# A conformer and state-space block on one core: partial sums of the down projection placed in the accumulation banks, and a fixed order for two kinds of activation in the mixers

## The chip, the cores and the metric

The kernel runs on one core of one Trainium2 chip. The metric is the device time of one execution in microseconds (us), taken as the median of several runs. TensorE (PE in the profile) multiplies matrices; PEld is its weight load, VectorE is DVE, ScalarE is ACT, GpSimd is POOL, and SyncE (SP) issues loads. "POOLq", "SPq" and "ACTq" are the issue queues of DMA transfers.

## The reference, cut to what matters

One transformer-like block on 512 tokens and 1024 channels, all in float32:

```python
h = rms_norm(x, mix_pre_g)
proj = h @ w_in                       # value/gate of a convolution branch, z, xbc, dt, gates
conv_out = conformer_conv_branch(...) # gated, 31-tap depthwise convolution, layer norm, SiLU, product
ssm_out = ssd_branch(z, xbc, ...)     # 8 groups: 4-tap convolution and SiLU, decay exponentials, gating by silu(z)
mixed = (g_conv * conv_out + g_ssm * ssm_out) @ w_out
x = x + rms_norm(mixed, mix_post_g)
h = rms_norm(x, ffn_pre_g)
gt, up = split(h @ w_gate_up)         # hidden width 2816
f = (silu(gt) * up) @ w_down
x = x + rms_norm(f, ffn_post_g)
```

## The kernel before

Each float32 operand is split into a high and a low half; `mm3` (L181) issues three matmuls for one product (high by high, high by low, low by high). Weights come in strips of 128 by 1024: `w_raw` (L139) loads a strip through SP's queue into one of five "raw" buffers (two more late in the kernel), ACT copies the high half out of it (`whi`, `chi`), and the low half is made in one of two ways: DVE subtracts the high half from the raw strip, or ACT writes minus the high half and POOL issues a DMA that adds the strip from memory to it. The list `ORDER` says in which sequence the strips are loaded.

The program is written with a framework that records each instruction with its operands, decides the order of every engine's queue at compile time by a list scheduler that follows the written order and its own estimate of when operands are ready, and adds all waits. `not_before(a, b)` (L176) adds an ordering edge for that scheduler between two instructions of one engine, with no wait on the chip. At run time every engine works through its queue in order.

Three places matter here.

**The mixers** (the loop from L701 over the eight groups `g`). In each group PE forms `x`, `B` and `C` strips (`proj_x`, `proj_bc`), each followed on DVE by three taps of a four-tap convolution and on ACT by a SiLU (`conv4`, L512). `make_L` (L403) loads a table of cumulative decays through POOL's queue, masks it on POOL (L410), and applies sixteen exponentials of 128 by 128 on ACT (L416). `proj_z1` and `proj_zz` form the gate `z` and apply SiLUs straight from the accumulation banks (L547, L567, L568). ACT holds one set of function tables at a time: an `ACT_TABLE_LOAD` stands ahead of the first function of another set. Between all this, DVE works off the taps of the 31-tap convolution in portions, `conv_some(n)` (L421).

**The end of the state-space branch.** After the last group `gate("gs", i)` (L735) forms six gate strips; each `gate` ends with `conv_some(TAPS_GATE)`, five taps. Then `s4` (L668) transposes the last group's result on PE, writes its high half `yh` on ACT and its low half `yl` on DVE (L679), and `ssm_out` (L685) multiplies it with the output weights, in four quarters of two products each.

**The down projection.** The first sixteen 128-row strips of `w_down` are taken as four 2 by 2 block products (`NS2 = 4`) with seven half-size products instead of eight; the seven are named P, T, S, p, Q, q, s, and `STEPS` (L103) lists them with their index `j` in the order in which PE does them. A step `k` is an ordinary strip. `prep(key)` (L1237) makes a step's operands on DVE and ACT, `S_AHEAD = 5` steps ahead of its use; `go(key)` (L1333) issues its products. `quad` (L1312) is one step on PE: 12 matmuls of 128 by 512. Each pair of banks collects one sum: A (P, then p), C (T, then q), B (S), D_2 (Q), and B2 (s). After the last P, S and Q the sums are read out into `parts[0..2]`, and the loop at the end (L1400) finishes each of four token tiles: the last strips, adding or subtracting a part (`extra`, L1409), mean square on ACT (`mean_sq`), the product with the gain on DVE (L1412), `factor` (DVE, then a power on POOL), scaling and store.

Of the kernel before, what the change touches and what calls it, by code (L numbers as in the profile page):

```python
# [18 lines left out]
P = 128  # L19
T = 512  # L20
# [82 lines left out]
STEPS = [("P", 0), ("P", 1), ("T", 0), ("P", 2), ("S", 0), ("T", 1), ("P", 3), ("S", 1)]  # L103
STEPS += [("p", 0), ("T", 2), ("p", 1), ("S", 2), ("p", 2), ("T", 3), ("p", 3), ("S", 3)]
STEPS += [("Q", 0), ("Q", 1), ("q", 0), ("Q", 2), ("q", 1), ("Q", 3), ("q", 2)]
STEPS += [("s", 0), ("k", KS2), ("q", 3), ("s", 1), ("k", KS2 + 1), ("s", 2), ("k", KS2 + 2), ("s", 3)]
BLOCKS = {"P": ((1, 0),), "T": ((1, 1),), "S": ((1, 2),), "p": ((1, 3),), "Q": ((2, 1), (2, 2)), "s": ((2, 3),)}
# [14 lines left out]
def block_kernel(ctx: ExitStack, tc: tile.TileContext, x, xT, x0, prm, hp, gp, w, out):  # L122
# [279 lines left out]

    def make_L(g, first=None):  # L403
        L = ssd.tile([P, HG, NT, P], F32, tag="L", bufs=2, name=f"L{g}")
        Lf = L.rearrange("p h c l -> p (h c l)")
        src = scr[HG * g : HG * (g + 1)].rearrange("h c l -> (h c l)").partition_broadcast(P)
        load = pool.dma_start(Lf, src)
        if first:
            not_before(load, first)
        pool.affine_select(  # L410
            out=Lf, in_=Lf, compare_op=ALU.is_ge, fill=-1e30, base=0,
            pattern=[[0, HG * NT], [1, P]], channel_multiplier=-1,
        )
        for c in range(NT):
            for h in range(HG):
                act.activation(L[:, h, c, :], L[:, h, c, :], AF.Exp, bias=nacs[:, c, HG * g + h : HG * g + h + 1])  # L416
        return L
# [94 lines left out]
    def conv4(ps, i, name):  # L512

        a = xbc_tile(name)
        act.activation(a, ps, AF.Identity, scale=col("ssm_w", i * KS + KS - 1), bias=col("ssm_b", i))  # L515
        for d in range(1, KS):
            dve.scalar_tensor_tensor(  # L517
                out=a[:, d:], in0=ps[:, : T - d], scalar=col("ssm_w", i * KS + KS - 1 - d),
                in1=a[:, d:], op0=ALU.mult, op1=ALU.add,
            )  # L520
        act.activation(a, a, AF.Silu)
        return a
# [11 lines left out]
    def proj_z1():  # L534
# [3 lines left out]
        for t2 in range(2):  # L538
# [8 lines left out]
            act.activation(z[:, 2 * t2 : 2 * t2 + 2, :], ps.rearrange("p (a b) -> p a b", a=2), AF.Silu)  # L547
        st[1]["z"] = z

    def proj_zz(g):  # L550
# [7 lines left out]
        for t in range(NT):  # L558
# [8 lines left out]
            act.activation(zb[t // 2][:, t % 2, :], ps[:, :GW], AF.Silu)  # L567
            act.activation(z[:, t, :], ps[:, GW:], AF.Silu)  # L568
# [166 lines left out]
    def gate(n, i, out_):  # L735
# [4 lines left out]
        conv_some(TAPS_GATE)  # L740
# [13 lines left out]
    gate("gs", 5, xbc_tile("sgs5"))  # L754
    s4(G - 1)
    ssm_out(G // 2 - 1, range(4))
# [480 lines left out]
    def prep(key):  # L1237
# [26 lines left out]
        elif kind == "p":  # L1264
            w_form(key, w_of(1, j, 3), seq["w1", 4 * j + 3])
            f_form(key, b21)
        elif kind == "Q":
# [4 lines left out]
        elif kind == "q":  # L1272
            dve.tensor_tensor(out=b11, in0=b11, in1=b21, op=ALU.add)
            w_form(key, w_of(2, j, 2), seq["w2", 4 * j + 2])
            f_form(key, b11)
        elif kind == "s":
            dve.tensor_tensor(out=keep[j], in0=keep[j], in1=w_of(2, j, 3), op=ALU.add)
            w_form(key, keep[j])
            f_form(key, b22)
# [28 lines left out]
    parts = [slot(tg, [P, 2, T], f"part{i}") for i, tg in enumerate(("b22h", "b22l", "t4h"))]  # L1308
# [3 lines left out]
    def quad(key, ps, start, stop, more=False):  # L1312

        (wh, wl), (fh, fl) = Wd[key], F_[key]
        for i in range(2):
            c = slice(i * T, (i + 1) * T)
            for e in range(2):
# [6 lines left out]
    at_b = [(turn["big"] - 3 + e) % 8 for e in range(2)]  # L1324
    B2 = []

    def f_step(t, k, n):
        (wh, wl), c, before = Wd["k", k], slice(n * T, (n + 1) * T), mark["pe3"]
        fh, fl = [f[:, t % 2, t // 2 * P : (t // 2 + 1) * P] for f in F_["k", k]]
        m = mm3(ps[t][n], fh, fl, wh[:, c], wl[:, c], False, k == NF - 1, ps[t][n] not in B2)  # L1330
        not_before(m, before)

    def go(key):  # L1333
# [9 lines left out]
        elif kind == "S":  # L1343
            quad(key, B, first_, last_)
            if last_:
                for e in range(2):
                    dve.tensor_tensor(out=parts[0][:, e], in0=B[e], in1=parts[0][:, e], op=ALU.add)
                for e in range(2):
                    dve.tensor_tensor(out=parts[1][:, e], in0=C[e], in1=parts[0][:, e], op=ALU.subtract)
        elif kind == "p":  # L1350
            quad(key, A, False, False, True)
        elif kind == "Q":
            quad(key, D_2, first_, last_)
            if last_:
                for e in range(2):
                    dve.tensor_tensor(out=parts[2][:, e], in0=parts[0][:, e], in1=D_2[e], op=ALU.subtract)
        elif kind == "q":
            quad(key, C, False, False, True)
        elif kind == "s":
            if first_:  # L1360
                B2.extend(yd_tile(at_b[e], f"tm_b2{e}") for e in range(2))
                ps.update({1: (B2[0], D_2[0]), 3: (B2[1], D_2[1])})
            quad(key, B2, first_, False)
# [5 lines left out]
    ps = {0: (A[0], C[0]), 2: (A[1], C[1])}  # L1369
# [12 lines left out]
    for t, tg in zip((1, 3, 0, 2), KEEP):  # L1382
# [3 lines left out]
    extra = {  # L1386
        (1, 0): (parts[2][:, 0], ALU.add), (3, 0): (parts[2][:, 1], ALU.add),
        (1, 1): (parts[1][:, 0], ALU.add), (3, 1): (parts[1][:, 1], ALU.add),
        (0, 1): (parts[0][:, 0], ALU.subtract), (2, 1): (parts[0][:, 1], ALU.subtract),
    }  # L1390

# [8 lines left out]
    for t in (1, 3, 0, 2):  # L1400
        mg = [w2.tile([P, T], F32, tag=tg, bufs=2, name=f"mg_{tg}{t}") for tg in ("dhi", "dlo")]
        ss = []
        for n in (1, 0):
            for k in range(KS2 + 3, NF):
                f_step(t, k, n)
            of = ps[t][n]
            if (t, n) in extra:
                by, op = extra[t, n]
                dve.tensor_tensor(out=mg[n], in0=of, in1=by, op=op)  # L1409
# [91 lines left out]
```

## Time and profile before

| what | us |
|---|---|
| median of three runs (1040.8 to 1042.3) | 1042.24 |
| the profiled execution's own time | 1039.82 |
| its span, first to last instruction | 1038.0 |
| PE busy | 1022.0 |
| DVE busy | 805.8 |
| ACT busy | 632.0 |
| POOL busy | 99.8 |

The profile is of one execution. A timeline row has the start, the duration, the engine, the line, the operation with the tiles it writes and reads, the shapes, a count of merged instructions and, in brackets, idle time of the engine just before it with what ended it. A row of waits has the waiting instruction, the one that released it, the sum in us, how often, and the longest. A row of stretches has, for the stretch, busy us and count of instructions of each engine, then TensorE's granted clock as a share of full speed, the busy share of the DMA engines and GB/s. A group row has its busy time and the mean ns of one, then the idle time before and what ended it. A matmul of 128 by 512 is shown with 0.39 us, but they overlap: the next one starts 0.23 us later.

### The profile page before, as it was taken

How to read it: one execution, taken by the hardware profiler on the slowest of the kernel's cores; microseconds unless marked ns; L12 is line 12 of the kernel's file. 1: busy time of each engine (PE TensorE's matmuls, PEld its weight loads, DVE VectorE, ACT ScalarE, POOL GpSimd, SP SyncE). 2: the span in 40 equal slices, each digit the busy share in tenths (PEclk: the TensorE clock that was granted, in tenths of full speed). 3: DMA queues.
4: the chain of work that ended last, by engine and by line, in shares of the span. 5: the costliest groups of instructions: out<-in, count | busy, mean ns of one | idle time of the engine just before them, and what ended most of it. 6: DMA issues, size and time to landing. Idle time of an engine off the chain costs nothing.

```text
span 1038.0 us, 15741 instructions
## 1 busy us (share of the span) xinstructions
PE 1022.0 (98%) x6101; PEld 885.9 (85%) x6101; DVE 805.8 (78%) x1172; ACT 632.0 (61%) x1047; POOL 99.8 (10%) x124
## 2 busy tenths in 40 slices
PE   9999999999999999999999999999999999999996
PEld 7898889878888888888878888889999999988785
DVE  7899976968595969597976455479997887897925
ACT  7655988684867476735432582376665664785712
POOL 0102101110111011101100000010000000010101
PEclk9999999999999999999999999999999999999999
DMA  8567634656456554544433223434565354488902
GB/s 295 155 167 227 144 91 134 184 133 173 119 144 159 131 145 134 157 128 121 119 106 102 81 79 105 162 110 135 164 185 160 106 164 138 143 219 267 304 21 81
DMA packets 43034, 152.91 MB, mean 147 GB/s; under 512 B 4944, under 2 KB 5968, under 8 KB 41936
## 3 DMA queue, kind: packets, MB, share of 16 engines
q1 hardware_dynamic: 30960, 105.71, 29.9%
q0 software_dynamic: 9792, 39.85, 19.5%
q10 hardware_dynamic: 2208, 6.36, 1.8%
q8 instruction: 48, 0.79, 0.3%
q14 instruction: 26, 0.21, 0.1%
HBM read 147.64 MB, written 4.26 MB: 146 GB/s over the span
## 4 chain that ended last, share of the span: by engine, by line
PE 78%; issue 7%; DVE 6%; ACT 4%; DMA 2%; POOL 1%; SPq 0%; POOLq 0%; DVEq 0%; ACTq 0%
PE xy L183 3%; PE xy L184 3%; PE xy L185 3%; PE pso L184 3%; PE pso L185 3%; PE pso L183 3%; PE px L185 2%; PE px L183 2%; PE px L184 2%; PE yv L184 2%; PE pz L184 2%; PE yv L183 2%; PE pz L183 2%; PE yv L185 2%; PE pz L185 2%
## 5 line engine op out<-in xcount | busy, mean ns | idle before, releaser
L149 ACT CAST whi<-raw 128x1024 fp32r<-128x1024 f32 (+2 forms) x116 | 115.1, 1004 | 161.4 <-PE pso L184 40.1
L433 DVE SCALAR_TENSOR_TENSOR a<-v,prm_t,a 128x511 f32<-128x511 f32 (+15 forms) x240 | 180.5, 754 | 10.6 <-ACT a L430 7.9
L155 DVE TENSOR_TENSOR wlo<-raw,whi 128x1024 fp32r<-128x1024 f32 (+2 forms) x76 | 86.1, 1136 | 48.5 <-ACT whi L149 46.1
L153 POOL DMA_DIRECT2D wlo<-in_w x40 | 35.8, 894 | 359.4 <-ACT wlo L152 125.3
L184 PE MATMUL pz<-wlo,hhi 128*128 128x512 f32 (+2 forms) x160 | 56.2, 352 | 0.5 <-DVE wlo L155 0.5
L185 PE MATMUL pz<-whi,hlo 128*128 128x512 f32 (+2 forms) x160 | 56.3, 352 | 0.0
L183 PE MATMUL pz<-whi,hhi 128*128 128x512 f32 (+2 forms) x160 | 55.9, 356 | 0.0
L184 PE MATMUL pso<-yl,whi 128*128 128x512 f32 x128 | 50.0, 390 | 1.4 <-DVE yl L679 1.4
L183 PE MATMUL px<-hhi,whi 128*128 128x512 f32 x128 | 50.2, 392 | 0.0
L917 ACT CAST whi_g<-raw 128x1024 fp32r<-128x1024 f32 x40 | 41.3, 1054 | 14.4 <-DVE raw L948 7.4
L185 PE MATMUL pso<-yh,wlo 128*128 128x512 f32 x128 | 49.9, 390 | 0.0
L185 PE MATMUL px<-hhi,wlo 128*128 128x512 f32 x128 | 49.8, 389 | 0.0
L184 PE MATMUL px<-hlo,whi 128*128 128x512 f32 x128 | 49.8, 389 | 0.0
L183 PE MATMUL pso<-yh,whi 128*128 128x512 f32 x128 | 49.7, 393 | 0.0
L922 DVE TENSOR_TENSOR wlo_g<-raw,whi_g 128x1024 fp32r<-128x1024 f32 x34 | 41.2, 1220 | 5.1 <-ACT whi_g L917 5.0
L416 ACT ACTIVATE L<-L,nacs 128x128 f32<-128x128 f32 x128 | 40.1, 390 | 5.6 <-POOL L L410 5.4
L152 ACT ACTIVATE wlo<-whi 128x1024 fp32r<-128x1024 f32 x40 | 42.2, 1056 | 0.3
L517 DVE SCALAR_TENSOR_TENSOR x<-px,prm_t,x 128x511 f32<-128x511 f32 (+2 forms) x48 | 35.1, 743 | 1.4 <-ACT x L515 1.2
L184 PEld LDWEIGHTS pz<-wlo,hhi 128*128 128x128 f32 x160 | 30.1, 188 | 5.0 <-DVE wlo L155 1.3
L183 PEld LDWEIGHTS pz<-whi,hhi 128*128 128x128 f32 x160 | 30.1, 188 | 4.0
L185 PEld LDWEIGHTS pz<-whi,hlo 128*128 128x128 f32 x160 | 30.1, 188 | 3.7
L917 ACT CAST chi_g<-raw 128x1024 fp32r<-128x1024 f32 x24 | 24.9, 1052 | 10.1 <-PE yv L185 4.6
(684 smaller groups left out, 3358.4 us busy)
## 6 DMA issues: line engine op xcount, KB each, us to landing
raw<-in_w SPq DMA_DIRECT2D x188, 512.0 KB, 4.3
wlo<-in_w POOLq DMA_DIRECT2D x40, 512.0 KB, 5.7
L<-scr POOLq DMA_DIRECT2D x8, 1024.0 KB, 6.4
wlo_g<-in_w POOLq DMA_DIRECT2D x13, 512.0 KB, 8.2
clo_g<-in_w POOLq DMA_DIRECT2D x7, 512.0 KB, 6.4
xr<-in_x ACTq DMA_DIRECT2D x4, 512.0 KB, 5.7
x2d<-xr ACTq DMA_DIRECT2D x4, 512.0 KB, 2.6
xres<-x2d SPq DMA_DIRECT2D x4, 512.0 KB, 4.9
```

Source lines behind the costliest of these rows:

```text
L149: act.copy(hi[:, c], src[:, c])
L152: act.activation(lo[:, c], hi[:, c].bitcast(F32), AF.Copy, scale=-1.0)
L153: mark["lo"] = pool.dma_start(lo[:, c], w[n][:, c].bitcast(F32R), accum_op=ALU.add)
L155: mark["wlo"] = dve.tensor_tensor(out=lo[:, c], in0=src[:, c], in1=hi[:, c].bitcast(F32), op=ALU.subtract)
L183: mark["pe"] = pe.matmul(ps, lh, rh, start=start, stop=False, skip_group_check=more)
L184: pe.matmul(ps, lh, rl, start=False, stop=False, skip_group_check=more)
L185: mark["pe3"] = pe.matmul(ps, ll, rh, start=False, stop=stop, skip_group_check=more)
L416: act.activation(L[:, h, c, :], L[:, h, c, :], AF.Exp, bias=nacs[:, c, HG * g + h : HG * g + h + 1])
L433: return dve.scalar_tensor_tensor(out=va[j][:, d:], in0=vs[j][:, : T - d], scalar=col("dw_w", j * KC + KC - 1 - d), in1=va[j][:, d:], op0= ...
L517: dve.scalar_tensor_tensor(out=a[:, d:], in0=ps[:, : T - d], scalar=col("ssm_w", i * KS + KS - 1 - d), in1=a[:, d:], op0=ALU.mult, op1=ALU ...
L917: a_ = act.copy(hi, src)
L922: d_ = dve.tensor_tensor(out=lo, in0=src, in1=hi.bitcast(F32), op=ALU.subtract)
```

## The change

There are three edits.

In the **down projection** the sums are written into the accumulation banks in the middle of the work instead of being kept aside and added at the end. `C` gets C minus parts[0] by an ACT copy after the last S; `B` gets parts[0] minus D_2, and `D_2` gets D_2 plus parts[1], both by DVE after the last Q; q, s and the last strips then go on adding to these banks. The third part and the bank pair B2 are gone, and so are the six DVE instructions at the end (`extra`). The order of the steps changes: S3 stands ahead of p3, and Q2 ahead of q0. The sum of weights that step s needs is made in step p from the strip that p has loaded anyway (the fourth blocks of "w1" and "w2" hold the same data), so the four loads of "w2" for s are gone. The low half of q's weights is made by DVE and no longer by ACT and an adding DMA.

In the **mixers** every exponential of `make_L` and every SiLU of `conv4`, `proj_z1` and `proj_zz` gets an ordering edge to the one written before it.

At the **end of the state-space branch** the five taps behind the gate strip gs5 move behind the first quarter of the last `ssm_out`.

```diff
+    "P0 P1 T0 P2 S0 T1 P3 S1 p0 T2 p1 S2",
+    "p2 T3 S3 p3 Q0 Q1 Q2 q0 q1 Q3 q2 s0",
+    "k16 q3 s1 k17 s2 k18 s3",
...
-BLOCKS = {"P": ((1, 0),), "T": ((1, 1),), "S": ((1, 2),), "p": ((1, 3),), "Q": ((2, 1), (2, 2)), "s": ((2, 3),)}
+BLOCKS = {"P": ((1, 0),), "T": ((1, 1),), "S": ((1, 2),), "p": ((1, 3),), "Q": ((2, 1), (2, 2))}
...
+    def by_table(ins):
+
+        if "table" in mark:
+            not_before(ins, mark["table"])
+        mark["table"] = ins
...
-                act.activation(L[:, h, c, :], L[:, h, c, :], AF.Exp, bias=nacs[:, c, HG * g + h : HG * g + h + 1])
+                by_table(
+                    act.activation(L[:, h, c, :], L[:, h, c, :], AF.Exp, bias=nacs[:, c, HG * g + h : HG * g + h + 1])
+                )
...
-        act.activation(a, a, AF.Silu)
+        by_table(act.activation(a, a, AF.Silu))
...
-    gate("gs", 5, xbc_tile("sgs5"))
+    gate("gs", 5, xbc_tile("sgs5"), 0)
     s4(G - 1)
-    ssm_out(G // 2 - 1, range(4))
+    ssm_out(G // 2 - 1, (0,))
+    conv_some(TAPS_GATE)
+    ssm_out(G // 2 - 1, (1, 2, 3))
...
         elif kind == "p":
             w_form(key, w_of(1, j, 3), seq["w1", 4 * j + 3])
             f_form(key, b21)
+            dve.tensor_tensor(out=keep[j], in0=keep[j], in1=w_of(1, j, 3), op=ALU.add)
...
         elif kind == "q":
             dve.tensor_tensor(out=b11, in0=b11, in1=b21, op=ALU.add)
-            w_form(key, w_of(2, j, 2), seq["w2", 4 * j + 2])
+            w_form(key, w_of(2, j, 2))
             f_form(key, b11)
         elif kind == "s":
-            dve.tensor_tensor(out=keep[j], in0=keep[j], in1=w_of(2, j, 3), op=ALU.add)
             w_form(key, keep[j])
             f_form(key, b22)
...
                 for e in range(2):
                     dve.tensor_tensor(out=parts[1][:, e], in0=C[e], in1=parts[0][:, e], op=ALU.subtract)
+                    act.copy(C[e], parts[1][:, e])
...
-                    dve.tensor_tensor(out=parts[2][:, e], in0=parts[0][:, e], in1=D_2[e], op=ALU.subtract)
+                    dve.tensor_tensor(out=B[e], in0=parts[0][:, e], in1=D_2[e], op=ALU.subtract)
+                    dve.tensor_tensor(out=D_2[e], in0=D_2[e], in1=parts[1][:, e], op=ALU.add)
...
-            quad(key, B2, first_, False)
+            quad(key, B, False, False, True)
...
-            of = ps[t][n]
-            if (t, n) in extra:
-                by, op = extra[t, n]
-                dve.tensor_tensor(out=mg[n], in0=of, in1=by, op=op)
-                of = mg[n]
-            ss.append(mean_sq(of, pt, f"c{t}", n))
-            dve.tensor_tensor(out=mg[n], in0=of, in1=gpost1[:, cols2[n]], op=ALU.mult)
+            ss.append(mean_sq(ps[t][n], pt, f"c{t}", n))
+            dve.tensor_tensor(out=mg[n], in0=ps[t][n], in1=gpost1[:, cols2[n]], op=ALU.mult)
```

More of the change, by code (lines that the diff above doesn't have):

```diff
@@ L733, in block_kernel, with gate @@
     gates = {}
-    def gate(n, i, out_):
+    def gate(n, i, out_, taps_=TAPS_GATE):
         ps = mm_tile(f"p{n}{i}")
@@ L1307, in block_kernel, with quad @@
     pt = ctx.enter_context(tc.tile_pool(name="pt", bufs=1))
-    parts = [slot(tg, [P, 2, T], f"part{i}") for i, tg in enumerate(("b22h", "b22l", "t4h"))]
+    parts = [slot(tg, [P, 2, T], f"part{i}") for i, tg in enumerate(("b22h", "b22l"))]
     gpost1 = slot("t4l", [P, D], "gpost1")
     nc.scalar.dma_start(gpost1, gp[1].partition_broadcast(P))
-    def quad(key, ps, start, stop, more=False):
+    def quad(key, ps, start, stop, more=False, es=(0, 1)):
         (wh, wl), (fh, fl) = Wd[key], F_[key]
@@ L1316, in quad @@
             c = slice(i * T, (i + 1) * T)
-            for e in range(2):
+            for e in es:
                 tok = slice(e * P, (e + 1) * P)
@@ L1329, in f_step @@
         fh, fl = [f[:, t % 2, t // 2 * P : (t // 2 + 1) * P] for f in F_["k", k]]
[L1330 removed]
+        m = mm3(ps[t][n], fh, fl, wh[:, c], wl[:, c], False, k == NF - 1, True)
         not_before(m, before)
@@ L1367, in go @@
                     f_step(t, j, n)
-    ps = {0: (A[0], C[0]), 2: (A[1], C[1])}
+    ps = {0: (A[0], C[0]), 2: (A[1], C[1]), 1: (B[0], D_2[0]), 3: (B[1], D_2[1])}
     ahead = STEPS + [("k", k) for k in range(KS2 + 3, NF)]
```

26 lines of the change are left out of this document (8 added, 18 removed).

## The prediction

> **What bounds the kernel now.** I read first the page's span and busy times, then PE's waits, then the stretches in which PE is not full.
>
> ```profile
> span 1038.0 us, 15741 instructions
> PE 1022.0 (98%) x6101; PEld 885.9 (85%) x6101; DVE 805.8 (78%) x1172; ACT 632.0 (61%) x1047; POOL 99.8 (10%) x124
> ```
> ```profile
> PE tm_c L183 <- DVE part L1349: 2.3, 1, 2.3
> PE pso L184 <- DVE yl L679: 1.4, 1, 1.4
> ...
> PE pz L184 <- DVE wlo L155: 0.5, 1, 0.5
> ...
> PE pyT L677 <- ACT y L664: 0.3, 1, 0.3
> ```
> ```profile
> 208.00:234.00 26.00, 25.23 (x117) 20.39 (x116) 16.94 (x23) 21.72 (x42) 3.93 (x5) 1.00 0.56 138
> ...
> 520.00:546.00 26.00, 24.62 (x112) 19.98 (x111) 19.11 (x25) 8.31 (x10) 0.92 (x1) 1.00 0.40 109
> ...
> 962.00:988.00 26.00, 23.66 (x104) 19.17 (x104) 23.50 (x30) 19.20 (x25) 2.62 (x3) 1.00 0.91 282
> ...
> 1014.00:1040.00 26.00, 15.33 (x68) 12.33 (x66) 15.19 (x26) 5.72 (x16) 3.10 (x4) 0.87 0.22 81
> ```
>
> ```profile
> 1028.49 0.39 PE L183 MATMUL tm_a<-whi_g,fh_k 128*128 128x512 f32 x1
> 1028.72 0.39 PE L184 MATMUL tm_a<-wlo_g,fh_k 128*128 128x512 f32 x1
> 1028.94 0.39 PE L185 MATMUL tm_a<-whi_g,fl_k 128*128 128x512 f32 x1
> ```
>
> The kernel's last three matmuls: one starts every 0.23 us, so a step of 12 takes 2.74.
>
> PE is idle for 1038.0 - 1022.0 = 16.0 us in all, at a granted clock of 1.00 in the stretches that matter. The change takes no matmul away and adds none, so nothing outside these 16 us can be won, except by another order of PE's queue. Where they lie: 0.8 in the mixers (26.00 - 25.23), 1.4 at the end of the state-space branch, 2.3 in the down projection, and 24.0 - 15.33 = 8.7 in the last stretch, of which only what follows PE's last matmul counts. The change touches all four places. The rest (the start, the gate and up projection) it leaves alone.
>
> The profiled execution took 1039.82, 1.8 more than its span; it is 2.4 below the median of 1042.24 and 1.0 below the lowest run shown. I make the sum on the profiled one and carry the difference over to the median.
>
> **1. The end of the state-space branch.**
>
> ```profile
> 521.44 1.23 DVE L155 TENSOR_TENSOR wlo<-raw,whi 128x1024 fp32r<-128x1024 f32 x1 [2.65 <-ACT whi L149]
> 522.58 3.80 DVE L433 SCALAR_TENSOR_TENSOR a<-v,prm_t,a 128x495 f32<-128x495 f32 x5
> 526.29 0.75 DVE L679 SCALAR_TENSOR_TENSOR yl<-pyT,prm_t,yh 128x512 fp32r<-128x512 f32 x1
> ...
> 529.26 0.69 DVE L698 TENSOR_TENSOR so<-pso,so 128x512 f32<-128x512 f32 x1 [0.92 <-PE pso L185]
> ```
> ```profile
> 523.78 1.26 ACT L678 ACTIVATE yh<-pyT,prm_t 128x512 fp32r<-128x512 f32 x2
> ```
> ```profile
> 527.09 0.50 PE L184 MATMUL pso<-yl,whi 128*128 128x512 f32 x1 [1.38 <-DVE yl L679]
> ```
>
> `yh` is there from about 524.4 on, but DVE makes `yl` only at 526.29, behind five taps of 3.80/5 = 0.76 us. Counted in fives back from 526.29, one is the last of gs4 and four belong to gs5. Without gs5's, DVE is free at 523.4, `yl` waits for `yh` alone and ends at 524.4 + 0.75 = 525.2; PE needs it at 527.09 - 1.38 = 525.7. So the wait goes whole: -1.4. The five taps (3.8 us) come after the first quarter. DVE's queue there has idle spots (0.92 before the first sum of results), and a result of `ssm_out`, 12 matmuls of 0.23 = 2.7 us, has three banks in turn, so an evacuation may be some 5 us late. I put them at nothing; if that cover is gone they cost 3.8 - 2.7 = 1.1. Bounds: -1.4 to -0.3.
>
> **2. The down projection, wait at the first q.**
>
> ```profile
> 942.96 1.23 DVE L1269 TENSOR_TENSOR raw<-raw,raw 128x1024 f32<-128x1024 f32 x1 [2.15 <-DMA raw<-in_w]
> ...
> 947.68 1.23 DVE L1269 TENSOR_TENSOR raw<-raw,raw 128x1024 f32<-128x1024 f32 x1 [2.29 <-DMA raw<-in_w]
> ...
> 956.91 1.23 DVE L1269 TENSOR_TENSOR raw<-raw,raw 128x1024 f32<-128x1024 f32 x1 [0.46 <-DMA raw<-in_w]
> ...
> 961.00 1.22 DVE L1277 TENSOR_TENSOR keep<-keep,raw 128x1024 f32<-128x1024 f32 x1
> ...
> 966.82 1.28 DVE L1347 TENSOR_TENSOR part<-tm_b,part 128x512 f32<-128x512 f32 x2
> 968.02 1.28 DVE L1349 TENSOR_TENSOR part<-tm_c,part 128x512 f32<-128x512 f32 x2
> 969.21 1.21 DVE L1229 TENSOR_TENSOR wlo_g<-keep,whi_g 128x1024 fp32r<-128x1024 f32 x1
> ...
> 976.41 1.23 DVE L1277 TENSOR_TENSOR keep<-keep,raw 128x1024 f32<-128x1024 f32 x1 [2.50 <-DMA raw<-in_w]
> ...
> 982.76 1.28 DVE L1356 TENSOR_TENSOR part<-part,tm_d 128x512 f32<-128x512 f32 x2
> ```
> ```profile
> 968.84 0.47 PE L183 MATMUL tm_c<-whi_g,f_q 128*128 128x512 f32 x1 [2.34 <-DVE part L1349]
> ```
> ```profile
> 935.75 1.27 ACT L1340 COPY part<-tm_a 128x512 f32<-128x512 f32 x2 [0.48 <-PE tm_a L185]
> ```
>
> q0 adds to bank C, and must wait until DVE has read C (968.02). PE came at 968.84 - 2.33 = 966.51. The last S had ended two steps before, near 961: DVE read it six us late, because its queue was full of preparations, and these had stood before for strips that DMA had not brought (2.15 + 2.29 + 0.46 = 4.9 us).
>
> What the new order gives: S3 one step earlier and Q2 ahead of q0 put p3, Q0, Q1, Q2 between S3 and q0 instead of Q0, Q1. Two steps are 2 x 12 x 0.23 = 5.5 us more cover; PE reaches q0 at 966.51 + 2.74 = 969.25. What DVE gets ahead of the parts: the four sums of weights move from s into p. Two of them stood ahead of the parts anyway (961.00 is one), so two are new: 2 x 1.14 = 2.3 us (1.22, less the overlap with the next, as from 521.44 to 522.58 above). The low half of q0's weights: 1.1. What it loses there: q1's preparation, which is five steps ahead no longer: 0.6 + 1.1 + 0.6 = 2.4. Net +1.0, so the parts end at 969.2 + 1.0 = 970.2 if DMA brings nothing sooner. Then the ACT copy into C, 1.27 for both banks by the only copy of that size shown (out of a bank, not into one): the first bank at about 970, the second 0.6 later. The wait would be about 1.2.
>
> ```profile
> q1 hardware_dynamic: 3203, 11.68, 57.8%
> q0 software_dynamic: 932, 3.36, 30.8%
> ```
>
> These are the DMA queues of 935 to 990 us: packets, MB, share of all DMA engines' time. The loads cost 57.8% x 55 / 11.68 = 2.7 us a MB, the adding DMAs 30.8% x 55 / 3.36 = 5.0. Four loads and four adding DMAs of 0.52 MB go: 2.1 x 2.7 + 2.1 x 5.0 = 16 us of the 49 that the DMA engines are busy here. The strips for Q2 and later then come sooner, and some of the 4.9 us of DVE's waiting goes; the waits at 942.96 and 947.68 also simply absorb the sums moved into p. I take the wait at q0 as 0.3 instead of 2.3: -2.0. Bounds: -2.3 (no wait) to +1.2 (two sums and their strips held longer, the first wait unrelieved: 3.5 instead of 2.3).
>
> [...]
>
> **3. The down projection, a new wait at the first s.** B is written from D_2 after Q3, and s0 needs it one step (2.74) after Q3. Before, DVE read D_2 at 982.76; s0 began at 982.66 in a fresh bank. If DVE stays as late, s0 waits 0.1 + 0.64 = 0.7 for the first bank and, with D_2's own sum in between, 1.3 for the second. But DVE had lost 2.50 us for s3's strip at 976.41, which is not loaded any more, and two sums of 1.14 that moved away; it gets two subtractions for q2 and q3. That is some 2.5 us of room: I take +0.2. Bounds: 0 to +1.3.
>
> **4. The tail.**
>
> ```profile
> 1029.92 0.63 ACT L853 ACTIVATE jk_c<-mg_dlo 128x512 bf16<-128x512 f32 x1 [3.90 <-DVE mg_dlo L1409]
> ...
> 1030.96 0.60 ACT L853 ACTIVATE jk_c<-tm_a 128x512 bf16<-128x512 f32 x1 [0.32 <-ACT jk_c L853]
> ```
>
> PE's last matmul ends at 1028.94 + 0.39 = 1029.33. ACT could square the last bank then, but it begins at 1030.96: it does the other half first, which waited until 1029.92 for DVE's addition of a part. Without that addition the other half is squared as soon as its bank is done, at about 1027.3, two us before the last one. The last square begins at 1029.4: 1.6 earlier, and all behind it (product, factor, power on POOL, scaling, store) moves with it. -1.6. Bounds: -1.0 (a store of the tile before in DVE's way: one 0.6 more) to -1.9.
>
> **5. The mixers.**
>
> ```profile
> L416 ACT ACT_TABLE_LOAD x19 | 24.4, 1283 | 0.3
> L521 ACT ACT_TABLE_LOAD x14 | 18.0, 1283 | 0.3
> ```
> ```profile
> L149 ACT CAST whi<-raw 128x1024 fp32r<-128x1024 f32 (+2 forms) x116 | 115.1, 1004 | 161.4 <-PE pso L184 40.1 <-PE pC L184 22.3 <-PE pgs L184 21.8
> ```
>
> In written order each group needs one load for its exponentials and one for its SiLUs: 8 + 8 instead of 19 + 14, so ACT saves some 17 x 1.28 = 22 us. ACT is busy 632 of 1038 and hardly delays PE: of its waits only 0.8 us lie here, and the 0.5 among them wait for a weight half of DVE. I take -0.3. Bounds: -0.8 to +1.5 (a table load's worth of one cast that comes late). What covers the sixteen exponentials in one block: the casts of weights behind them. By the group row the casts wait for PE to give back a strip, 161.4 us in all, so they are strips ahead.
>
> [...]
>
> **Sum:** -1.4 - 2.0 + 0.2 - 1.6 - 0.3 = -5.1. The profiled execution would go from 1039.8 to 1034.7, the median from 1042.24 to 1037.1.
>
> **The rivals.**
>
> *A, the wait only moves* (17%). DVE is not sooner at the parts, q0 waits 1.2 to 3.5, s0 as much as above. Then 2 and 3 cancel and the rest stays: -1.4 - 1.6 = -3.0, 1039.2. For it speaks that DVE is busy 23.50 of 26 there; against it the 5.5 us of cover.
>
> *B, nothing that can be told* (12%). The scheduler lists other queues around the edits. Tail and `yl` win 3.0, and new waits of the same kind and size as those now in the list (2.3 the longest) take it back: about 1042.
>
> *C, slower: DVE's lateness feeds itself through the raw buffers* (13%). Place: p0 to the parts. The sum that moves into p makes DVE the last reader of p's strip, where ACT's cast was; a buffer comes free later, so the next load starts later, and DVE stands for it. If the four sums count whole (4.6 instead of 2.3) and DVE's 4.9 us of standing for strips doubles, the parts come at 969.2 + 1.0 + 2.3 + 4.9 = 977.4 and q0 waits 978.0 - 969.25 = 8.8: +6.4 against before; with 1.3 at s0 and the 3.0 won elsewhere, +4.7: 1047. It decides from the point where q0's wait passes 2.3 + 3.0 = 5.3. For it: the DMA share of 0.91, and the three waits. Against: the adding DMAs gone, and DVE's standing absorbs work first.
>
> That the mixers' edit does nothing (the loads don't fall in number) would cost the 0.3 only.
>
> **How the numbers follow.** Forecast 58%: 1037.1, its own range 1035 to 1039. All bounds at their best: -1.4 - 2.3 - 1.9 - 0.8 = -6.4, 1035.8, and runs scatter by 1.5 (1040.8 to 1042.3): low 1034.3. The high end takes in A and half of B: 1041.8. A measurement of this kernel can tell about 0.2%, 2.1 us. Faster by more: the forecast and A, 75%; within it: B, 12%; slower: C, 13%.
>
> **What would show it.** PE's waits: `pso` on `yl` gone; `tm_c` under 1 us, and behind DVE `part` or an ACT copy; a wait of `tm_b` on DVE (0 to 1.3). The last square of ACT starts within 0.2 us of PE's last matmul, and the span ends some 7 us after it instead of 8.7. Table loads of L416 and L521 at 16 to 20 together. Strips of L145 are four fewer, adding DMAs of L1227 four fewer. I am wrong if PE's idle time grows between 940 and 990, if the tail does not shorten, or if waits of PE for ACT or for weight halves appear in the mixers.

## The result, and the profile after

| | median, us | runs | range |
|---|---|---|---|
| before | 1042.27 | 4 | 1040.8 to 1044.42 |
| after | 1032.12 | 4 | 1031.56 to 1032.59 |

The ratio is 0.9901 (95% interval 0.9883 to 0.9919): 10.15 us gone, twice the 5.1 of the forecast, and below the range. The profiled execution took 1032.06, its span is 1030.3. The span of before's profiled execution was 1038.0, so from trace to trace only 7.7 have gone; the other 2.4 are the distance of that execution from before's median.

Some executions of most kernels here take about 6 us longer than the others (27 of 92 later ones of before, at a median of 1048.3 instead of 1042.7), in the traces all of it between 730 and 940 us, so where about half of a kernel's runs are such I also give the median of the lower ones, and the profiles of down_only, dma_kept, hold2 and old_order are of the longer kind.

The page's first lines, PE's waits, the ACT table loads among the groups, and the four stretches that answer to those of before (the last one again ends with the span):

```profile
span 1030.3 us, 15679 instructions
PE 1020.2 (99%) x6101; PEld 886.6 (86%) x6101; DVE 803.8 (78%) x1172; ACT 602.2 (58%) x1024; POOL 94.6 (9%) x120
```
```profile
PE warm_ps L270 <- DVE woken L265: 1.0, 1, 1.0
PE xy L186 <- DVE f L1107: 0.9, 2, 0.5
PE v L187 <- DVE t1l L1041: 0.4, 1, 0.4
PE yv L186 <- ACT f L1170: 0.2, 1, 0.2
```
```profile
L426 ACT ACT_TABLE_LOAD x8 | 10.3, 1283 | 0.1
L532 ACT ACT_TABLE_LOAD x8 | 10.3, 1283 | 3.2 <-DVE x L528 3.1
```
```profile
208.00:234.00 26.00, 26.00 (x121) 21.55 (x120) 13.46 (x18) 21.13 (x47) 3.93 (x5) 1.00 0.61 162
520.00:546.00 26.00, 26.00 (x120) 21.23 (x119) 19.02 (x26) 7.96 (x9) 0.92 (x1) 1.00 0.39 105
962.00:988.00 26.00, 26.00 (x116) 21.40 (x115) 21.23 (x26) 13.66 (x19) 0.00 (x0) 1.00 0.32 110
1006.00:1032.00 26.00, 17.17 (x76) 13.85 (x74) 11.40 (x20) 5.51 (x16) 2.19 (x4) 0.91 0.22 81
```

`tm_c`, `pso`, `pz` and `pyT` have left the list of waits: PE is full in the first three stretches. The table loads at these two lines are 16, against 19 + 14. In both traces a load, of 1283 ns, stands ahead of an exponential, SiLU or sigmoid wherever the one before it on ACT was of another of these three kinds, 52 times in before and 31 in after, and besides only once, at the start. The DMA share of 962 to 988 has fallen from 0.91 to 0.32.

The down projection and the tail, in order of time, from the timeline of after:

```profile
955.36 1.28 DVE L1357 TENSOR_TENSOR part<-tm_b,part 128x512 f32<-128x512 f32 x2
956.56 1.27 DVE L1359 TENSOR_TENSOR part<-tm_c,part 128x512 f32<-128x512 f32 x2
...
957.27 1.19 ACT L1360 COPY tm_c<-part 128x512 f32<-128x512 f32 x2 [0.48 <-DVE part L1359]
...
965.52 0.39 PE L186 MATMUL tm_c<-chi_g,f_q 128*128 128x512 f32 x1
...
1022.79 0.39 PE L188 MATMUL tm_a<-whi_g,fl_k 128*128 128x512 f32 x1
...
1023.45 0.60 ACT L866 ACTIVATE jk_c<-tm_a 128x512 bf16<-128x512 f32 x1 [1.54 <-PE tm_a L188]
```

The parts begin 11 us sooner than before (966.82), where the prediction had them end 1.0 later (970.2 instead of 969.2). Of the 11, 3.6 are PE's own lead when it comes to these steps; counted from the same matmul of step P3 (PE's 5700th) the parts begin 23.8 us later, in before 31.7. The copies into C end at 957.27 + 1.19 = 958.46, and q0 starts at 965.52: 7 us are to spare. From the end of PE's last matmul (1022.79 + 0.39) to the end of the span are 1030.3 - 1023.2 = 7.1 us, where before had 1038.0 - 1029.3 = 8.7. A single copy of 128 by 512 on ACT takes 0.591 into a bank (after) and 0.586 out of one (before); the 1.19 and 1.27 of the merged rows differ only in how closely the second follows the first.

### The profile page after: what moved, and what is told of

The parts are those of the page before. It is cut to its first block, busy times and chain, and to the rows that moved or that the text cites. A ratio compares the mean times of both kernels' runs of the same rounds, so it can differ in the third digit from the quotient of the medians.

```text
span 1030.3 us, 15679 instructions
## 1 busy us (share of the span) xinstructions
PE 1020.2 (99%) x6101; PEld 886.6 (86%) x6101; DVE 803.8 (78%) x1172; ACT 602.2 (58%) x1024; POOL 94.6 (9%) x120
## 4 chain that ended last, share of the span: by engine, by line
PE 91%; DVE 4%; ACT 2%; issue 1%; POOL 0%; ACTq 0%; POOLq 0%; DVEq 0%
PE xy L186 3%; PE xy L187 3%; PE xy L188 3%; PE pz L187 3%; PE pz L188 3%; PE pz L186 3%; PE pso L186 3%; PE pso L187 3%; PE px L188 3%; PE pso L188 3%; PE px L186 3%; PE px L187 3%; PE yv L186 2%; PE yv L187 2%; PE yv L188 2%; PE yd L636 2%
```

## The experiments

In the terms of the expectations, "theory T" is: listed waits, a granted clock that before loses behind its wait at the first q, and a wait in the mixers that many executions of before have and the first profile had not. Theory D looks for the whole surplus in the down projection, M for a part of it in the mixers, S in the chip or the moment.

### What each edit brings alone

The kernel before once more, and with one edit of the three at a time, on one chip.

> The kernel before, unchanged. Its profiled execution took 1039.8, the median of its runs 1042.3, up to 1044.4; the changed kernel's runs all lie within 1.0 of each other. Theory D (the down projection): what differs from run to run is how long PE waits at the first q, since the loads there fill the DMA engines; a slower execution then shows a wait of tm_c on DVE part above 2.3 us, by as much as its span is above 1038.0. Rival M (the mixers): the wait of tm_c stays at 2.3 and PE's waits between 100 and 530 us grow instead. Rival S (neither; the chip or the moment): this chip shows about 1040 with all waits of PE as in the first profile.

> The down projection's edit alone. In the traces it is worth 2.6 at the first q and 1.6 in the tail. D: it also takes away the 2.4 by which the runs lie above the profiled one: 1042.3 - 6.6 = 1035.7, ratio 0.9937, and its runs lie within 1.5 of each other. M or S: 1042.3 - 4.2 = 1038.1, ratio 0.9960, under M with the scatter of before (3 to 4 us).

> The edges between exponentials and SiLUs alone. In the traces worth 1.8 to 2.0, nearly all near 205 to 225 us, where two waits of PE (0.5 and 0.3 as listed) go. D or S: 1042.3 - 1.9 = 1040.4, ratio 0.9982, scatter as before. M: 1042.3 - 1.9 - 2.4 = 1038.0, ratio 0.9959, scatter under 1.5. In its profile some 15 to 17 table loads fewer at L416 and L521 (their lines move by a few) and neither wait.

> The five taps moved behind the first quarter, alone. By the traces 1.6 (the wait of pso on yl was listed with 1.4): 1040.7, ratio 0.9985, under D, M and S alike. If a wait cost only what the list gives, 1.4. If the taps were paid back behind the first quarter, under 0.5.

The edits are the three of the diff, each alone; before_again alters nothing.

| | median, us | ratio to before, 95% interval | lower runs |
|---|---|---|---|
| before_again | 1043.01 | 1.0002, 0.9981 to 1.0022 | |
| down_only | 1039.62 | 0.9949, 0.9925 to 0.9973 | six of 1036.04 to 1037.43, median 1036.8 |
| mixers_only | 1041.3 | 0.9968, 0.9946 to 0.999 | seven of 1037.66 to 1041.74, median 1040.3 |
| taps_only | 1041.55 | 0.9964, 0.9941 to 0.9987 | |

PE's waits in before_again:

```profile
PE tm_c L183 <- DVE part L1349: 2.0, 1, 2.0
PE pyT L677 <- ACT y L664: 1.8, 1, 1.8
PE pso L184 <- DVE yl L679: 1.4, 1, 1.4
```

The second profile of the same kernel is not the first: `pyT` waits 1.8 for ACT, where the first showed 0.3 (and 0.5 of `pz`). taps_only and down_only show 1.8 as well, mixers_only none. before_again gives a ratio of 1.0002, so S falls; the down projection's edit is the largest part, about 6 us in its lower runs, but the other two bring more than the 1.7 that the prediction gave them together, so D alone does not do either.

Of before_again, the stretches around the first q, and PE's timeline from its wait on:

```profile
964.00:968.00 4.00, 3.65 (x17) 2.68 (x15) 3.87 (x5) 4.00 (x6) 0.98 (x2) 1.00 0.87 307
968.00:972.00 4.00, 2.39 (x6) 1.95 (x7) 4.00 (x7) 3.97 (x6) 0.13 (x1) 0.70 1.02 251
972.00:976.00 4.00, 4.00 (x17) 3.25 (x16) 2.66 (x3) 1.91 (x3) 0.89 (x1) 0.87 1.05 299
```
```profile
969.61 0.75 PE L183 MATMUL tm_c<-whi_g,f_q 128*128 128x512 f32 x1 [1.96 <-DVE part L1349]
970.16 0.63 PE L184 MATMUL tm_c<-wlo_g,f_q 128*128 128x512 f32 x1
970.58 0.63 PE L185 MATMUL tm_c<-whi_g,f_q 128*128 128x512 f32 x1
971.01 0.63 PE L183 MATMUL tm_c<-whi_g,f_q 128*128 128x512 f32 x1
...
973.34 0.39 PE L183 MATMUL tm_c<-whi_g,f_q 128*128 128x512 f32 x1
973.57 0.39 PE L184 MATMUL tm_c<-wlo_g,f_q 128*128 128x512 f32 x1
```

Behind the wait of 1.96 the matmuls start every 0.43 us instead of 0.23, until 973.1, and the granted clock is 0.70 and 0.87. No wait lists this: PE counts as busy. From the wait on, 24 starts in a row took 1.7 us more than 24 x 0.228. So the wait at the first q costs about twice what it is listed with. mixers_only (3.5 of wait) lost 2.7 behind it, taps_only (2.8) 1.7. The first profile of before, with 2.34 of wait, lost 0.1 and kept a clock of 1.00: an exception among executions of before, since its mean clock of 0.998 is reached by only 4 of the 92 later runs of before (most have 0.995 or 0.996), while the changed kernel and down_only have 0.998 or 0.999 in all.

mixers_only and taps_only also show that the edits do not simply add up. In mixers_only PE comes 3.9 us sooner to the down projection than in before_again, but the parts do not come sooner by as much: the wait grows from 2.0 to 3.5 and the loss behind it from 1.7 to 2.7, and only 1.3 of the 3.9 are left at the end. In taps_only 1.6 become 0.4. And the wait of `pso` on `yl` is gone in mixers_only as well, with the five taps in their old place. Its DVE there:

```profile
516.75 1.23 DVE L155 TENSOR_TENSOR wlo<-raw,whi 128x1024 fp32r<-128x1024 f32 x1
517.89 5.34 DVE L439 SCALAR_TENSOR_TENSOR a<-v,prm_t,a 128x497 f32<-128x497 f32 x7
523.35 0.75 DVE L685 SCALAR_TENSOR_TENSOR yl<-pyT,prm_t,yh 128x512 fp32r<-128x512 f32 x1
```

Before, DVE stood 2.65 us for ACT's `whi` ahead of the last `wlo` (at 521.44); here it doesn't, and is through the taps in time. So either edit alone removes this wait. Whether the five taps' place is worth anything beside the mixers' edges was not run; by this trace it is not (PE takes 74.5 us from its 2600th to its 3000th matmul in mixers_only, in taps_only and in after, and 76.1 in before).

### What in the down projection does it

after_again alters nothing. dma_kept and dma_less are:

```diff
 after, to dma_kept
-            dve.tensor_tensor(out=keep[j], in0=keep[j], in1=w_of(1, j, 3), op=ALU.add)   # in step p
-            w_form(key, w_of(2, j, 2))
+            w_form(key, w_of(2, j, 2), seq["w2", 4 * j + 2])
+            dve.tensor_tensor(out=keep[j], in0=keep[j], in1=w_of(2, j, 3), op=ALU.add)   # in step s
```
```diff
 before, to dma_less
-STEPS += [("p", 0), ("T", 2), ("p", 1), ("S", 2), ("p", 2), ("T", 3), ("p", 3), ("S", 3)]
+STEPS += [("p", 0), ("T", 2), ("p", 1), ("S", 2), ("p", 2), ("T", 3), ("S", 3), ("p", 3)]
+            dve.tensor_tensor(out=keep[j], in0=keep[j], in1=w_of(1, j, 3), op=ALU.add)   # in step p
-            w_form(key, w_of(2, j, 2), seq["w2", 4 * j + 2])
+            w_form(key, w_of(2, j, 2))
-            dve.tensor_tensor(out=keep[j], in0=keep[j], in1=w_of(2, j, 3), op=ALU.add)   # in step s
```

> The changed kernel once more, nothing altered. Theory T (the gain is the listed waits, 5 to 6 us, plus the clock that before loses behind its wait at the first q, plus a 1.8 us wait in the mixers that most executions of before have): the granted clock is 0.998 or more in every run; the lowest runs are 1031.5 to 1033; about a third of the runs lie some 6 us higher, 1037 to 1039, as they do for before and for the down projection's edit alone, because nothing in the change touches that. Rival U (the change also removes that second level): no run above 1034.

> The changed kernel, but the low half of q's weights is again made by ACT and an adding DMA, and the four w2 strips for s are loaded and summed in step s again, so that the DMA engines keep their load of before; the order of the steps and the sums in the banks stay new. By the order alone (two steps, 5.5 us more cover for the parts) there is no wait at the first q above 0.5 us and the time is within 1.5 of the changed kernel's own. Rival (the relief of the DMA engines is what brought the parts forward): the first q waits 1 to 4 us, the granted clock dips behind it, and the time is 3 to 6 above the changed kernel's.

> The kernel before, with the relief of the DMA engines and S3 one step earlier (S3 ahead of p3, the sum of s's weights made in p from the strip that is there, the low half of q's weights on DVE); Q2 stays behind the first q, and the parts are added at the end as before, with no sum written into a bank. If earlier strips and one step of cover (2.7 us) are enough: no wait of tm_c above 0.5, granted clock 0.998 or more, 3 to 4 us below before (about 1038.5 to 1039.5), the tail 8.7 as before, the pso and pyT waits as before. Rival: the wait at the first q stays at 1 or more and the time within 1.5 of before.

after_again: 1032.71 (0.9906, 0.9882 to 0.9929), five runs of 1031.96 to 1033.27 and one of 1039.32; rival U falls. dma_kept: 1042.97 (0.9998, 0.9979 to 1.0016), no gain left at all. dma_less: 1037.88 (0.9946, 0.993 to 0.9962), six runs within 1.4 us.

dma_kept, PE's one long wait, and DVE's queue from its timeline:

```profile
PE tm_b L186 <- DVE tm_b L1367: 7.0, 1, 7.0
```
```profile
966.23 1.23 DVE L1290 TENSOR_TENSOR keep<-keep,raw 128x1024 f32<-128x1024 f32 x1 [1.33 <-DMA raw<-in_w]
...
969.71 1.28 DVE L1357 TENSOR_TENSOR part<-tm_b,part 128x512 f32<-128x512 f32 x2
...
979.29 1.23 DVE L1290 TENSOR_TENSOR keep<-keep,raw 128x1024 f32<-128x1024 f32 x1 [5.36 <-DMA raw<-in_w]
...
990.26 0.69 DVE L1367 TENSOR_TENSOR tm_b<-part,tm_d 128x512 f32<-128x512 f32 x1
```

The new order does what the prediction wanted of it: the first q does not wait, although the parts are about as late as before (969.71; counted from the same matmul of P3, 30.9 us later, in before 31.7). But the same lateness then meets the first s, where B must be written: 7.0 us. With the sums and the DMA load left in place, the order only moves the wait. The expectation of the order alone had the first q right and the time wrong; the rival had the sign, but neither the place nor the size (10.7 above after's 1032.3, where it said 3 to 6). In dma_less, with the old place of Q2 and no sum in a bank, no wait of `tm_c` is left.

Four more kernels take the relief and the order apart. old_order puts Q2 behind the first q again, q_by_dma gives q's low half back to ACT and the adding DMA, loads_kept loads the four strips of s again without using them, and strips_only is before with nothing but the sum for s moved into p (and S3 ahead of p3, as p adds to what S makes).

```diff
 after, to old_order
-    "p2 T3 S3 p3 Q0 Q1 Q2 q0 q1 Q3 q2 s0",
+    "p2 T3 S3 p3 Q0 Q1 q0 Q2 q1 Q3 q2 s0",
 after, to q_by_dma
-            w_form(key, w_of(2, j, 2))
+            w_form(key, w_of(2, j, 2), seq["w2", 4 * j + 2])
 after, to loads_kept
+            again = w_of(2, j, 3)[:, :1]            # in step s
+            pool.tensor_scalar(out=again, in0=again, scalar1=1.0, scalar2=None, op0=ALU.mult)
 dma_less, to strips_only
-            w_form(key, w_of(2, j, 2))
+            w_form(key, w_of(2, j, 2), seq["w2", 4 * j + 2])
```

> The changed kernel with Q2 behind the first q again (S3 stays ahead of p3), so one step of cover, 2.7 us, is taken from the parts. The changed kernel's parts and copies are done 7 us before the first q, so by theory T (the relief of DMA brought them forward) 4.3 us are left and the time is the changed kernel's, within 0.6. By the prediction's step 2 (the order is what hides the parts) a wait of 1 to 2.5 us comes back, and with the clock behind it the time is 1034 to 1037.

> The changed kernel, but the low half of q's weights is made by ACT and an adding DMA again; the four w2 strips for s stay away. It parts the relief of the DMA engines in two. If the four adding DMAs are the greater half of it (2.1 MB at 5.0 us a MB against 2.1 at 2.7, by the prediction): strips come late again, DVE stands for them by 3 us or more, a wait of 1 to 4 us shows at the first s or the first q, and the time is 1035 to 1038. If the four strips of s, with their sums in DVE's queue, are what holds it up: no wait above 0.5 in the down projection, and the time within 1 us of the changed kernel's.

> The changed kernel, but the four w2 strips for s are loaded again, at their old place in the sequence of loads; nothing is made of them but that POOL multiplies one column by 1.0, and the sum for s is still made in p. If the DMA engines' load and the raw buffers are what held DVE up: strips behind these come late, DVE stands for them, the first s or the first q waits several us, and the time is that of the run that kept strips and sums, near 1043. If it was DVE standing in its queue at the sums, whose strips had not come: no wait above 0.5 in the down projection and the time within 1 of the changed kernel's, 1032 to 1033.5.

> The kernel before with the sum for s made in p and the four w2 strips gone (for that S3 must stand ahead of p3, since p adds to what S makes); the low half of q's weights stays with ACT and the adding DMA, the parts are added at the end, the mixers and the five taps are as before. If the strips of s alone carry the gain: the wait of tm_c gone, granted clock 0.997 or more, and the time that of the run in which q's low half moved too, 1037.5 to 1038.5. If the adding DMAs matter as well in the old order: a wait of tm_c of 1 or more, 1040 to 1043.

| | median, us | ratio to before, 95% interval | lower runs |
|---|---|---|---|
| old_order | 1033.32 | 0.9919, 0.9886 to 0.9951 | four of 1032.79 to 1033.37 |
| q_by_dma | 1032.58 | 0.9894, 0.9868 to 0.9919 | all six |
| loads_kept | 1032.99 | 0.9901, 0.9871 to 0.9932 | all four |
| strips_only | 1041.15 | 0.9967, 0.9941 to 0.9993 | six of 1037.06 to 1038.84, median 1037.8 |

None of the four shows a wait in the down projection. So neither Q2's place nor the adding DMAs nor the four loads, each put back alone, bring the wait back (by the lower runs they cost 0.3 to 0.8); strips_only, in its lower runs, has the whole gain of dma_less (1037.88). loads_kept, its DMA queues of 935 to 990 us and DVE's timeline at the parts:

```profile
q1 hardware_dynamic: 3033, 11.04, 53.6%
```
```profile
954.53 1.22 DVE L1283 TENSOR_TENSOR raw<-raw,raw 128x1024 f32<-128x1024 f32 x1
955.67 1.28 DVE L1359 TENSOR_TENSOR part<-tm_b,part 128x512 f32<-128x512 f32 x2
```

It loads 11.04 MB there (before 11.68, after 8.93) and still has its parts at 955.67, directly behind the fourth sum for Q. In before there were ten us between these two (956.91 and 966.82), filled with preparations and with the sums for s at 961.00 and 965.08. In loads_kept it is POOL that stands for these strips, and nothing waits for POOL.

Counted from the same matmul of P3, the parts begin 31.3 to 32.9 us later in the four traces with before's down projection, 30.9 in dma_kept, and 23.3 to 24.1 in all others. Where the 8 us go is seen in strips_only, which keeps the adding DMAs and Q2's old place:

```profile
954.90 1.22 DVE L1270 TENSOR_TENSOR raw<-raw,raw 128x1024 f32<-128x1024 f32 x1
...
957.84 1.22 DVE L1229 TENSOR_TENSOR clo_g<-raw,chi_g 128x1024 fp32r<-128x1024 f32 x1
958.98 1.28 DVE L1347 TENSOR_TENSOR part<-tm_b,part 128x512 f32<-128x512 f32 x2
```

The fourth sum for Q comes 2.0 us sooner, and between it and the parts lie 4.1 us of DVE's queue instead of 9.9: the two sums for s (2.3) are gone from there, and 3.5 us of preparations are now listed behind the parts. In before DVE did not stand at those two sums themselves (961.00 has no idle time before it); it stood at the strips for Q ahead of them, and behind the parts, at 976.41, for a strip of s. In dma_kept it stands for the sums' own strips, 1.33 ahead of the parts and 5.36 behind them.

That the sums in DVE's queue are the cause is therefore likely, but not shown to the end. Only before's down projection and dma_kept have the adding DMAs and the four loads together (14.2 to 15.2 and 15.0 MB moved between 935 and 990 us); all others move 13.0 MB or less. A kernel with both transfers and without the sums was not run, so a DMA load of which either half alone does no harm is a rival that stands.

### What a wait costs, and where the mixers' gain comes from

hold6 and hold2 put six, or two, multiplications by 1.0 between the parts and the copies into C. mixers_off is after without the ordering edges of the mixers.

```diff
 after, to hold6 (hold2 with range(2))
+                for _ in range(6):
+                    pool.tensor_scalar(out=parts[1], in0=parts[1], scalar1=1.0, scalar2=None, op0=ALU.mult)
+                for e in range(2):
                     act.copy(C[e], parts[1][:, e])
 after, to mixers_off
     def by_table(ins):
-        if "table" in mark:
-            not_before(ins, mark["table"])
-        mark["table"] = ins
+        return ins
```

> The changed kernel with six multiplications by 1.0 on POOL over parts[1] put between the parts and the ACT copies into C, so that the first q waits by what POOL takes beyond the 7 us that are free there. Theory T: with a wait of 2 us or more the granted clock falls below 1.00 in the next 4 to 8 us, the matmuls there start more than 0.23 us apart, and the loss against the changed kernel is the listed wait plus 1.5 to 2.6 us. Rival (a wait costs what is listed, plus at most 0.3): clock 1.00 behind the wait, and the loss equals the listed wait.

> The changed kernel with two multiplications by 1.0 on POOL over parts[1] ahead of the copies into C, where the run before had six (4.35 us each, 19.0 us of wait): the first q should wait 19.0 - 4 x 4.35 = 1.6 us. Theory T: a wait of this size is enough, in most executions, to halve the granted clock for some 3 us after it, and the loss against the changed kernel is 1.6 + 0.25 + 1.2 to 2 = 3 to 4 us (1035.4 to 1036.4). Rival: the clock stays at 1.00 at so short a wait, and the loss is 1.6 to 1.9 (1034.0 to 1034.3).

> The changed kernel without the mixers' ordering edges; the down projection and the five taps as changed. Theory T (the mixers' edit removes a wait of 1.8 us at pyT that most executions of before have, not 0.3): 2 to 3 us above the changed kernel, 1034.3 to 1035.3, with a wait of pyT on ACT of 1.8 or waits of pz and pSa in the profile. The prediction's step 5 (0.3): 1032.6.

hold6: 1053.93 (1.0098, 1.0082 to 1.0114), with a listed wait of 19.0: 21.6 above after's 1032.3 (the median of its nine lower runs). hold2: 1038.91 (0.9968, 0.9944 to 0.9992), lower runs at a median of 1038.0, with a listed wait of 2.8 where I had expected 1.6 (its two multiplications took 10.0 us, by the 4.35 of hold6's they would have taken 8.7): 5.7 above after. PE's waits and the stretches of hold2:

```profile
PE tm_c L186 <- ACT tm_c L1363: 2.8, 1, 2.8
```
```profile
972.00:976.00 4.00, 1.23 (x6) 0.72 (x5) 0.00 (x0) 0.85 (x2) 3.03 (x2) 1.00 0.34 132
976.00:980.00 4.00, 4.00 (x12) 3.10 (x11) 3.16 (x5) 3.22 (x5) 0.00 (x0) 0.57 0.00 0
980.00:984.00 4.00, 4.00 (x19) 3.30 (x18) 4.00 (x6) 3.49 (x6) 0.00 (x0) 1.00 0.00 0
```

From 976 to 980 only 12 matmuls start, at a clock of 0.57. A wait of 2.8 and one of 19.0 lose about the same behind them: the 24 starts from the wait on took 1.7 and 1.9 more than at full speed. Theory T stands; by the rival hold2 would have been 2.8 above after, not 5.7 (of the 5.7, wait and clock account for 4.5 in the profiled execution; the rest was not followed).

mixers_off: 1035.13 (0.9943, 0.9917 to 0.9968), seven lower runs of 1033.87 to 1035.21 at a median of 1034.5, so 2.2 above after. Its wait of `pyT`, and ACT's timeline in it and in after:

```profile
PE pyT L686 <- ACT y L673: 1.8, 1, 1.8
```
```profile
205.94 3.04 ACT L424 ACTIVATE L<-L,nacs 128x128 f32<-128x128 f32 x10 [3.42 <-POOL L L417]
208.99 1.28 ACT L530 ACT_TABLE_LOAD   x1
...
210.92 1.28 ACT L424 ACT_TABLE_LOAD   x1
...
218.50 1.69 ACT L673 ACTIVATE y<-y,rs 128x256 f32<-128x256 f32 x4
```
```profile
215.64 1.71 ACT L675 ACTIVATE y<-y,rs 128x256 f32<-128x256 f32 x4
...
225.59 1.28 ACT L426 ACT_TABLE_LOAD   x1
226.88 1.28 ACT L426 ACTIVATE L<-L,nacs 128x128 f32<-128x128 f32 x4
```

Without the edges ACT begins the next group's exponentials at 205.94, when POOL's mask happens to be done, and goes back and forth between two tables; `y`, for which PE waits, comes at 218.50. With them the block stands behind everything of this group, at 225.59, and `y` comes at 215.64. The start of the exponentials hangs on POOL: in the first profile of before they began at 205.00 and `y` came at 217.56, 0.9 earlier than in mixers_off; there PE waited 0.3. Of the seven profiles without these edges four show 1.8 and three 0.3. From the profile of mixers_off to that of after PE comes 2.9 sooner out of the mixers, 2.6 of it by 240 us. That is more than the wait at `pyT`. From its 900th to its 2600th matmul PE takes 295.1 to 296.3 us in the seven profiles without the edges and 293.3 to 294.2 in the nine with them: 1.9 less in the mean, of which 1.2 is idle time. The other 0.7 lies in matmuls that start closer together and was not followed.

## Why the prediction fell short

The median of the lower runs from kernel to kernel (different chips, so a few tenths are loose):

| step | from, to | us | by the traces, at its place | predicted |
|---|---|---|---|---|
| sum for s and its loads out of the late steps, S3 earlier | 1042.7 (before), 1037.8 (strips_only) | -4.9 | -4.0 | -2.0 |
| sums in the banks, tail | 1037.8, 1036.8 (down_only) | -1.0 | -1.3 | -1.4 |
| five taps later | 1036.8, 1034.5 (mixers_off) | -2.3 | -1.6 | -1.4 |
| mixers' order | 1034.5, 1032.3 (after) | -2.2 | -2.9 | -0.3 |

The sum is 10.4, for a measured 10.15. The traces' column starts from before_again; its sum is 9.8, and from span to span 10.1 have gone. In it the first step has 3.8 at the first q and 0.2 in the tail; the 0.9 that the medians have more cannot be laid to this edit, since strips_only's profile is also 1.1 sooner out of the mixers, which the edit doesn't touch (`pyT` happens to wait 0.3 there). The shares of the last two steps hang on their order, as either removes the wait of `pso`.

**The first q** was mis-sized, and for a wrong reason. The mechanism (DVE late, and a wait at bank C) was right, and the wait is gone. But the prediction took "0.3 instead of 2.3", a wait at its listed length, in a profiled execution that happened not to lose its clock. From before_again to strips_only PE gains 2.1 at the first q and 1.7 more, by the clock, up to the first s: 3.8 for a term of 2.0. No row of waits shows the second, so "nothing outside these 16 us can be won" failed as well: PE's busy time held it. And the step put the cover down to the order ("Two steps are 2 x 12 x 0.23 = 5.5 us more cover") and the relief mostly to the adding DMAs. dma_kept shows that order without relief is worth nothing, q_by_dma that putting the adding DMAs back costs nothing; strips_only, which moves the sums and drops their loads, has the whole gain. The step counted these sums as moved work ("two are new: 2 x 1.14 = 2.3 us") and concluded that the parts come 1.0 later. Against PE's own steps they came 8 sooner: the waits for Q's strips did absorb the sums moved into p, as it said they might, and the parts then stood ahead of 5.8 us of sums and preparations that had been ahead of them.

**The mixers** were mis-sized: "of its waits only 0.8 us lie here" was true of one execution. In four of seven profiles `pyT` waits 1.8. The bound of -0.8 was that execution's too. Even against that execution, which waits 0.8 there, PE comes 2.0 sooner out of the mixers in after, so the listed waits were not the bound that the step took them for. The 17 x 1.283 = 21.8 us of table loads saved don't come back as time; what the traces show to come back is one `y` that is no longer behind the next group's exponentials, and closer starts of the matmuls.

**The carry-over to the median** was the step that hid both. It treated the 2.4 us between the profiled execution and the median as a constant, "I make the sum on the profiled one and carry the difference over". The profiled execution was below all three timed runs. What it lacked, by the trace of before_again, a halved clock (1.6 more) and 1.2 more in the mixers (1.8 at `pyT` in place of 0.3 and 0.5), less a wait at the first q that is 0.4 longer, was part of what the change removes, so the difference did not carry over: after's profiled execution (1032.06) lies at its median (1032.12).

**Right:** the tail, -1.6 predicted and 8.7 to 7.1 in the traces; `pso` on `yl` gone, 1.4 predicted, and 1.6 by the traces (taps_only's PE is 0.05 us later than before_again's ahead of this place and 1.56 sooner behind it), though the mixers' edges alone do it too; the new wait at the first s, predicted +0.2 and 0; table loads, 16. The five taps cost nothing later. Rival A (the wait only moves) did not come about, but dma_kept shows it to be real: with the four sums and the DMA load left in place, the wait moves to the first s and grows to 7.0. Rival C fell: with the sum in p no wait of PE grew in the down projection.

**Open:** in the first step, whether the sums in DVE's queue or the two halves of the DMA load together made the parts late, and how much belongs to S3's earlier place, which could not be parted from it, since the sum in p needs what S makes; in the mixers, the 0.7 of closer starts.

## What to carry to other kernels

A wait of TensorE in the middle of full work can be worth more than its listed length (here six of seven waits from 1.96 us up lost another 1.7 to 2.7): look at the granted clock and at the distance of the matmuls' starts in the 4 us behind it. Before a sum is made on one profiled execution, compare it with the timed runs: if it lies below all of them, the median has losses that this profile does not show, and these are likely to sit at the same places. For a queue worked in order, ask of each instruction not what it takes but what it stands for and what is listed behind it: moving four sums to where their operand already lay, and dropping their loads, was worth 4.0 us in the traces, though that engine was not spared a single instruction. And a gain ahead of a late engine is partly lost at the place where it is late, as in mixers_only: repair that place first, or measure the edits together.

## What the runs showed of the hardware that was not expected

**Half the clock behind six of seven waits from 1.96 us up.** A wait of 1.96 us was enough in before_again: the granted clock is 0.70 and 0.87 in the two stretches of 4 us from 968 on. The starts then come every 427 ns instead of 229, eight of them in before_again, hold2 and dma_kept to twelve in mixers_only (clock 0.50 from 968 to 972 us): 8 x 0.427 = 3.4 us, 12 x 0.427 = 5.1. Waits of 1.82 (`pyT`, four traces) and 1.38 (`pso`, in before_again and four others) are followed by a clock of 1.00 (down_only, 208 to 234 and 520 to 546 us). The slow spell doesn't always begin at once: in hold2 the first three starts behind the wait are still at or near full speed (0.33, 0.23 and 0.32 us to the next), and in the first profile of before none is slow after 2.34 (0.1 lost over 24 starts, clock 1.00). Why the clock dropped behind 1.96 and not behind 2.34 was not shown.
